# Block 1's left operand from a host-transposed copy of x, and the first keys' transposes three units later

## The chip, the core and the metric

The kernel runs on one core of one Trainium2 chip. The metric is the device time of one execution in microseconds. Engines are named as in the profile: PE (matrix multiply; PEld is its weight load), DVE, ACT, POOL and SP, which here only issues DMAs. "Lnnn" is a line of the kernel before.

## The reference

A decoder block ("block 1": attention of two kinds, then a large mixture of experts) is followed by two more attention layers, on 256 tokens of width 1024. The change touches the start of block 1 alone:

```python
h = rms_norm(x, attn_norm[i])                 # x: 256 x 1024
proj = h @ w_in[i]                            # w_in: 1024 x 3072
mq, mk, mv, dq, dk, dv = jnp.split(proj, split_pts, axis=-1)
mq = apply_rope(rms_norm(mq, q_norm_moba[i]), cos, sin)     # the same for mk, dq, dk
...
x = x + mixed @ w_out[i]                      # mixed: both attentions' outputs
```

## The kernel before

**Units.** Every weight matrix streams through PE in float32 that is split in two parts: `wh` (rounded by ACT, L119) and `wl` (the rest, subtracted by DVE, L129). A unit is 1024 columns of one such pair, and three products (L219 `wh·xh`, L220 `wl·xh`, L221 `wh·xl`) of four 128x512 pieces each, 12 matmuls in all. In block 1, units 0 to 3 make dk (the keys of the second attention), 4 to 7 dq, 8 to 11 mk, 12 to 15 mq, 16 to 19 dv, 20 to 23 mv, and 24 to 31 the output projection. A 1 MB load `raw` holds two units; three `raw` buffers stand, four of `wh` and of `wl`. `Stream.loads` issues the load of chunk c on SP when the parts of chunk c-3 are made. The first chunk comes in four pieces, the second in two, and `after(n)` puts other loads between them.

**The left operand.** x lies with tokens on partitions. `make_xT` transposes it on PE (L270, 16 transposes by the constant `ident`), and ACT (L288) and DVE (L289) make `xh` and `xl` of it with the gain. While these data come, PE runs matmuls on zeros: `busy(15)`, then `busy(36)` behind the first four transposes (`WARM`). The norm of x (`norms`: squares on ACT L247, a chain of 13 small operations on DVE L249, L226 to L233, L465, L466) is only needed after the product, as a scale per token; it ends in `rx` and `rx2`.

**After a product.** `qk` takes a finished dk, dq, mk or mq in two halves of 128 tokens (`part`): ACT squares (L528), DVE multiplies by the rope tables (L532, tiles `mc` and `ms`) and sums the squares (L538), POOL joins the rope (L541, L542). When both halves are there, `norm` runs on POOL: L549, the chain of `rsqrt` (L226 to L236) and, for keys alone, the scaling of `mc` by L557 and L559. Then PE transposes (`tr`, L570, eight 128x128) and ACT copies (L573). `score` (L607) multiplies transposed queries and keys.

**Order.** Each engine runs its own list, in the order in which the program calls. What does not belong to the products is hung on unit numbers, with halves: `self.at(delay, fn)` runs `fn` when the unit counter has moved by `delay`. The table at the head of `block1` holds these numbers: TT the distance from a finished product to its transposes (queries, keys), XS the parts of `xh`, `xl` and the norm, SD the four scores of the second attention, CD the combination of its two maps. With TT = (3, 6), dk, finished when the counter stands at 4, is transposed at 10, and dq, finished at 8, at 11.

Of the kernel before, what the change touches and what calls it, by code (L numbers as in the profile page):

```python
# [18 lines left out]
P = 128  # L19
# [5 lines left out]
REACH = 64  # L25
KA = 16
NCAND = 50
WARM = (15, 36)
CAND = [16 // (a + 1) for a in range(16)]

FIELDS = {}
# [123 lines left out]
class Kernel:  # L155
# [200 lines left out]
    def build(self):  # L356
        tc, nc, A = self.tc, self.nc, self.A
        with (
            tc.tile_pool(name="main", bufs=1) as main,
            tc.tile_pool(name="raw", bufs=3) as raw,  # L360
            tc.tile_pool(name="wgt", bufs=4) as wgt,
            tc.tile_pool(name="ps", bufs=1, space=bass.MemoryType.PSUM) as ps,
            tc.manual_schedule(),
        ):
            self.main = main
            self.pspool = ps

            class _PS:
                @staticmethod
                def tile(shape, dtype, name, tag):  # L370
                    return ps.tile(shape, dtype, name=name, tag=tag, bufs=2 if tag == "s" else 1)

            self.ps = _PS
            x = main.tile([P, 2, 1024], F32, name="x")
            warm = main.tile([P, 1], F32, name="warm")
            nc.vector.memset(warm, 1.0)
            nc.scalar.activation(warm, warm, AF.Copy, scale=warm)

            zero = main.tile([P, 256], F16, name="zero")
            nc.vector.memset(zero, 0.0)  # L380
            idle = self.bank("a0")

            def busy(n):
                for _ in range(n):
                    nc.tensor.matmul(idle[:, 0:256], zero[:, 0:128], zero, start=True, stop=True)

            self.busy = busy
            busy(WARM[0])
            self.consts = [main.tile([P, NFIELD[0]], F32, name="consts0")]
            nc.sync.dma_start(self.consts[0], A["consts0"])  # L390
            xv = A["x"].rearrange("(t p) c -> p t c", p=P)
            nc.sync.dma_start(x[:, :, 0:256], xv[:, :, 0:256])

            srcs = []
            srcs += [A["w_in"][i] for i in range(12)]
            srcs += [A["w_out"][i] for i in range(4)]
            srcs += [A["peer_query"][i] for i in range(8)]
            dn = [A["peer_down"][i] for i in range(64)]
            up = [A["peer_up"][i * 256 : i * 256 + 256, :].rearrange("(j p) d -> p j d", p=P) for i in range(64)]
            srcs += dn[:50] + up[:8] + dn[50:58] + up[8:14] + dn[58:] + up[14:]  # L400
            srcs += [A["a_w_in"][i] for i in range(40)]
            srcs += [A["a_w_out"][i] for i in range(4)]
            srcs += [A["b_w_in"][i] for i in range(16)]
            srcs += [A["b_w_out"][i] for i in range(4)]
            with tc.tile_pool(name="b1c", bufs=1) as pool:
                self.consts.append(pool.tile([P, NFIELD[1]], F32, name="consts1"))

                def after(n):
                    if n == 2:
                        nc.sync.dma_start(self.consts[1], A["consts1"])  # L410
                        return
                    for c in ((1,), (2, 3))[n]:
                        cs = slice(c * 256, c * 256 + 256)
                        nc.sync.dma_start(x[:, :, cs], xv[:, :, cs])

                self.stream = Stream(nc, raw, wgt, srcs, 3, 3, after)
                self.block1(x)
            self.peer(x)
            self.layer_a(x)
            self.layer_b(x)  # L420
# [3 lines left out]
    def block1(self, x):  # L424
        tc, nc, A = self.tc, self.nc, self.A
        ident = self.const("ident")

        TT = (3, 6)
        XS = (1, 1, 1.5, 8)
        SD = (12, 13, 14, 15)  # L430
        CD = (15.5, 15.5, 19.5, 19)
        TD = (18.5, 19, 21, 20.5)
        PD = (20.5, 21, 22, 22)
        FD = (23, 23.5, 24.5, 25.5)
# [10 lines left out]
        with (  # L445
# [3 lines left out]
        ):  # L449
            xh = pl.tile([P, 8, 256], F32R, name="xh1")  # L450
            xl = pl.tile([P, 8, 256], F32R, name="xl1")
            steps = self.make_xT(xh, xl, x, self.small("g_attn"), ahead=0)
            steps[0]()
            self.busy(WARM[1])
            self.stream.prime(1)
# [59 lines left out]
            def qk(key, tabn):  # L515
                n = 64 if "moba" in tabn else 128
                r = 512 // n
                isq = tabn[0] == "q"

                def evac(b0, b1):  # L520
                    ss = pw.tile([P, 2, 8], F32, name=self.nm("ss"), tag="ss")
                    rk = pl.tile([P, 2, 8], F32, name="rk_" + key)
                    tm = pw.tile([P, 2, 8], F32, name=self.nm("tm"), tag="tm")
                    mt = []

                    def part(t, b):
                        sq = pw.tile([P, 512], F32, name=self.nm("sq"), tag="sq")
                        nc.scalar.activation(sq, b, AF.Square)  # L528
                        mc = pw.tile([P, 512], F32, name=self.nm("mc"), tag="mc", bufs=4)
                        ms = pw.tile([P, 512], F32, name=self.nm("ms"), tag="ms")  # L530
                        for dst, kk in ((mc, "c"), (ms, "s")):
                            nc.vector.tensor_tensor(  # L532
                                dst.rearrange("p (r n) -> p r n", n=n),
                                b.rearrange("p (r n) -> p r n", n=n),
                                tabs[tabn, kk][:, t, :].unsqueeze(1).to_broadcast([P, r, n]),
                                op=ALU.mult,
                            )
                        nc.vector.tensor_reduce(ss[:, t, :], sq.rearrange("p (h d) -> p h d", d=64), axis=AX.X, op=ALU.add)  # L538
                        mcv = mc.rearrange("p (h two f) -> p h two f", two=2, f=32)
                        msv = ms.rearrange("p (h two f) -> p h two f", two=2, f=32)  # L540
                        nc.gpsimd.tensor_tensor(mcv[:, :, 0, :], mcv[:, :, 0, :], msv[:, :, 1, :], op=ALU.subtract)  # L541
                        nc.gpsimd.tensor_tensor(mcv[:, :, 1, :], mcv[:, :, 1, :], msv[:, :, 0, :], op=ALU.add)  # L542
                        mt.append(mc)

                    def norm():

                        eng = nc.gpsimd
                        for t in range(2):
                            eng.tensor_scalar(ss[:, t, :], ss[:, t, :], rx2[:, t : t + 1], 0.5 * EPS, op0=ALU.mult, op1=ALU.add)  # L549
                        self.rsqrt(rk, ss, tm, eng)  # L550
                        for t in range(2):
                            if isq:
                                eng.tensor_scalar(
                                    rk[:, t, :], rk[:, t, :], rxs[0][:, t : t + 1], -0.125, op0=ALU.mult, op1=ALU.mult
                                )
                            else:
                                eng.tensor_scalar(rk[:, t, :], rk[:, t, :], rxs[0][:, t : t + 1], None, op0=ALU.mult)  # L557
                                v = mt[t].rearrange("p (h d) -> p h d", d=64)
                                nc.gpsimd.tensor_tensor(  # L559
                                    v, v, rk[:, t, :].unsqueeze(2).to_broadcast([P, 8, 64]), op=ALU.mult  # L560
                                )
                        RW[key] = rk

                    def tr(pp2):
                        def f():
                            pt = self.bank("s")
                            for j in range(2):
                                for t in range(2):
                                    c0 = (2 * pp2 + j) * 128
                                    nc.tensor.transpose(  # L570
                                        pt[:, j * 256 + t * 128 : j * 256 + t * 128 + 128], mt[t][:, c0 : c0 + 128], ident
                                    )
                            nc.scalar.copy(qT[key][:, 2 * pp2 : 2 * pp2 + 2, :].rearrange("p a b -> p (a b)"), pt)  # L573

                        return f

                    part(0, b0)
                    self.at(1, lambda: (part(1, b1), norm()))
                    for p2 in (1, 0):
                        self.at(TT[0] if isq else TT[1], tr(p2), True)  # L580

                return evac

# [1112 lines left out]
def layout(inputs):  # L1696
    i = {k: np.asarray(v) for k, v in inputs.items()}
    a = {}
    a["x"] = np.ascontiguousarray(i["x"][0])
    for n, c in enumerate(_consts(i)):  # L1700
        a[f"consts{n}"] = c
    a["w_in"] = _proj(i["w_in"][0], [4, 3, 1, 0, 5, 2])
# [57 lines left out]
```

## Time and profile before

| | us |
|---|---|
| runs, median of 3 (lowest, highest) | 1468.54 (1466.36, 1471.48) |
| the profiled execution, whole | 1466.31 |
| its span in the profile | 1464.5 |
| PE busy in the span | 1440.2 (98%) |
| PE busy in 10 to 60 us of the span | 43.82 of 50.00 |
| PE busy in 150 us to the end | 1303.98 of 1314.50 |

The profile is one execution. The span's first microseconds are the start of the program; all that the change touches lies in its first 110 us. "Idle before" in square brackets is the time in which an engine had nothing to run, and who released it.

### The profile page before, as it was taken

What the parts mean: (1) busy time and instruction counts of PE and PEld (TensorE: products, weight loads), DVE (VectorE), ACT (ScalarE), POOL (GpSimd) and SP (SyncE); (2) the same over time, 40 slices, a digit from 0 to 9 for tenths busy, and PEclk for the clock granted to TensorE, in tenths of its full rate; (3) what the DMA queues carried; (4) which work ended last, traced back from release to release, by engine and by line L of the source; (5) the groups of instructions that cost most, each with busy time, mean ns of one, the idle gap of its engine ahead of it and who ended that gap; (6) DMA issues with size and microseconds to landing.
All of it is one profiled execution on the core that took longest, in us unless ns stands there. A gap on an engine that the chain in (4) does not pass through costs nothing.

```text
span 1464.5 us, 24829 instructions
## 1 busy us (share of the span) xinstructions
PE 1440.2 (98%) x9375; PEld 1263.0 (86%) x9375; DVE 978.4 (67%) x1985; ACT 888.5 (61%) x1723; POOL 324.5 (22%) x626
## 2 busy tenths in 40 slices
PE   9889999999999999999999999999999999999998
PEld 7677999999999989999878888887888888887887
DVE  6666899996688854456989655556554666666444
ACT  5675554544688854446888544446666666665653
POOL 4760300000133300001333000006333543207300
PEclk9999999999999999999999999999999999999999
DMA  6334445455443355554334555554544454445432
GB/s 251 141 116 150 151 172 194 177 181 190 148 145 124 137 201 182 190 186 163 126 135 143 185 191 200 195 200 179 187 159 166 165 177 168 159 162 181 166 110 86
DMA packets 50935, 243.14 MB, mean 166 GB/s; under 512 B 4224, under 2 KB 11520, under 8 KB 31488
## 3 DMA queue, kind: packets, MB, share of 16 engines
q1 hardware_dynamic: 50528, 241.04, 46.4%
q8 instruction: 73, 1.20, 0.3%
q10 hardware_dynamic: 288, 0.52, 0.1%
q14 instruction: 46, 0.38, 0.1%
HBM read 240.50 MB, written 1.05 MB: 165 GB/s over the span
## 4 chain that ended last, share of the span: by engine, by line
PE 82%; ACT 8%; POOL 4%; DVE 2%; issue 2%; DMA 1%; SPq 0%; ACTq 0%; DVEq 0%; POOLq 0%
PE a L219 14%; PE a L221 14%; PE a L220 14%; PE s L219 10%; PE s L220 9%; PE s L221 9%; ACT o1l L926 4%; ACT wh L119 2%; PE s L1365 2%; PE o L1441 1%; PE o L1449 1%; PE s L1275 1%; DMA raw<-in_w_in_dram 1%; PE t L934 1%; PE o L934 1%
## 5 line engine op out<-in xcount | busy, mean ns | idle before, releaser
L129 DVE TENSOR_TENSOR wl<-raw,wh 128x1024 fp32r<-128x1024 f32 (+1 forms) x435 | 551.5, 1276 | 139.8 <-ACT wh L119 139.7
L119 ACT CAST wh<-raw 128x1024 fp32r<-128x1024 f32 (+1 forms) x435 | 453.0, 1043 | 257.7 <-PE a L221 188.0
L219 PE MATMUL s<-nh,wh 128*128 128x256 f32 x1024 | 292.5, 286 | 0.0
L220 PE MATMUL s<-nl,wh 128*128 128x256 f32 x1024 | 289.6, 283 | 0.0
L221 PE MATMUL s<-nh,wl 128*128 128x256 f32 x1024 | 289.5, 283 | 0.0
L923 POOL TENSOR_TENSOR o1h<-o,ghT 128x256 f16<-128x256 f16 x128 | 85.0, 664 | 561.8 <-DVE o L921 550.8
L219 PE MATMUL a<-wh,gh 128*128 128x512 f32 x512 | 202.4, 395 | 0.0
L221 PE MATMUL a<-wh,gl 128*128 128x512 f32 x512 | 199.4, 390 | 0.0
L220 PE MATMUL a<-wl,gh 128*128 128x512 f32 x512 | 199.3, 389 | 0.0
L219 PEld LDWEIGHTS s<-nh,wh 128*128 128x128 f32 x1024 | 196.9, 192 | 0.1
L220 PEld LDWEIGHTS s<-nl,wh 128*128 128x128 f32 x1024 | 196.4, 192 | 0.1
L221 PEld LDWEIGHTS s<-nh,wl 128*128 128x128 f32 x1024 | 196.2, 192 | 0.0
L926 ACT ACTIVATE o1l<-o,glT 128x64 f16<-128x64 f16 x512 | 146.5, 431 | 29.4 <-DVE o L921 26.4
L219 PE MATMUL a<-wh,xha 128*128 128x512 f32 x320 | 132.4, 414 | 0.5 <-DVE xha L282 0.5
L221 PE MATMUL a<-wh,xla 128*128 128x512 f32 x320 | 125.4, 392 | 0.0
L220 PE MATMUL a<-wl,xha 128*128 128x512 f32 x320 | 125.1, 391 | 0.0
L893 DVE TENSOR_TENSOR gl<-big,gh 128x512 fp32r<-128x512 f32 x64 | 44.3, 693 | 110.4 <-ACT gh L892 110.4
L221 PEld LDWEIGHTS a<-wh,gl 128*128 128x128 f32 x512 | 96.1, 188 | 20.5
L219 PEld LDWEIGHTS a<-wh,gh 128*128 128x128 f32 x512 | 96.6, 189 | 18.6
L220 PEld LDWEIGHTS a<-wl,gh 128*128 128x128 f32 x512 | 96.3, 188 | 18.8
L881 ACT ACTIVATE big<-s 128x512 f32<-128x512 f32 x64 | 38.3, 598 | 98.9 <-PE s L221 98.9
L1370 DVE CUSTOM_DVE_ANT_0 e<-s,bias 128x128 f32<-128x128 f32 (+2 forms) x128 | 34.1, 326 | 70.5 <-PE s L1365 70.5
(409 smaller groups left out, 2588.7 us busy)
## 6 DMA issues: line engine op xcount, KB each, us to landing
raw<-in_peer_down_dram SPq DMA_DIRECT2D x64, 1024.0 KB, 4.8
raw<-in_peer_up_dram SPq DMA_DIRECT2D x64, 1024.0 KB, 4.8
raw<-in_a_w_in_dram SPq DMA_DIRECT2D x40, 1024.0 KB, 4.8
raw<-in_b_w_in_dram SPq DMA_DIRECT2D x16, 1024.0 KB, 4.7
raw<-in_w_in_dram SPq DMA_DIRECT2D x10, 1024.0 KB, 4.9
raw<-in_peer_query_dram SPq DMA_DIRECT2D x8, 1024.0 KB, 4.8
raw<-in_w_out_dram SPq DMA_DIRECT2D x4, 1024.0 KB, 4.8
bias<-in_bias_dram SPq DMA_DIRECT2D x8, 512.0 KB, 5.9
```

The lines of the kernel that those rows point to most:

```text
L119: self.nc.scalar.copy(hi[:, c], self.part(u)[:, c])
L129: eng.tensor_sub(lo[:, c], self.part(u)[:, c], hi[:, c])
L219: nc.tensor.matmul(o, lh, rh, start=start, stop=False)
L220: nc.tensor.matmul(o, lh, rl, start=False, stop=False)
L221: nc.tensor.matmul(o, ll, rh, start=False, stop=stop)
L881: nc.scalar.activation(big[:, sl : sl + 2, :].rearrange("p a b -> p (a b)"), hb, AF.Gelu)
L893: nc.vector.tensor_sub(wl, big[:, sl : sl + 2, :], wh)
L923: nc.gpsimd.tensor_tensor(o1h, o1, b(ghT, H), op=ALU.mult)
L926: nc.scalar.activation(o1l[:, :, i], o1[:, :, i], AF.Copy, scale=glT[:, t : t + 1])
L934: nc.tensor.matmul(o, o2[:, :, i], o1h[:, :, i], start=True, stop=False)
L1365: nc.tensor.matmul(o, l, r, start=start, stop=stop)
L1370: nc.vector.tensor_tensor_reduce(e[:, c], s[:, c], bts[i][:, qt * w : qt * w + w], -1.0, 3.0e38, ALU.add, ALU.min, nmx[g][:, h, qt : qt + 1],)
```

## The change

The host adds an input `xT`, 128 partitions of 8 x 256: x transposed and laid out as `xh` wants it. `make_xT` and its 16 transposes are no longer called in block 1; ACT and DVE read `xT` from its tile in place of PE's banks. `busy(36)` becomes `busy(20)` and stands right behind `busy(15)`. At the head of SP's queue only eight columns of `consts0` stand (the gain); `xT` comes in pieces between the first weights (two, two and four of its eight slices), and x itself and the rest of `consts0` behind the second chunk's pieces and `consts1`. The norm of x moves from 1.5 to 2. dk's transposes move from 6 units after the product to 9; those of mk stay at 6, those of queries at 3. The scores move from (12, 13, 14, 15) to (14, 14.5, 15.5, 16), and `mc` has six buffers in place of four.

```diff
-WARM = (15, 36)
+WARM = (15, 20)
...
-            nc.sync.dma_start(self.consts[0], A["consts0"])
             xv = A["x"].rearrange("(t p) c -> p t c", p=P)
-            nc.sync.dma_start(x[:, :, 0:256], xv[:, :, 0:256])
+            G0, G1 = 128, 136
+            nc.sync.dma_start(self.consts[0][:, G0:G1], A["consts0"][:, G0:G1])
...
+                nc.sync.dma_start(self.xT[:, 0:2, :], xTv[:, 0:2, :])
...
                     if n == 2:
                         nc.sync.dma_start(self.consts[1], A["consts1"])
+                        nc.sync.dma_start(x, xv)
+                        nc.sync.dma_start(self.consts[0][:, 0:G0], A["consts0"][:, 0:G0])
+                        nc.sync.dma_start(self.consts[0][:, G1:], A["consts0"][:, G1:])
                         return
-                    for c in ((1,), (2, 3))[n]:
-                        cs = slice(c * 256, c * 256 + 256)
-                        nc.sync.dma_start(x[:, :, cs], xv[:, :, cs])
+                    ks = (slice(2, 4), slice(4, 8))[n]
+                    nc.sync.dma_start(self.xT[:, ks, :], xTv[:, ks, :])
...
-        TT = (3, 6)
-        XS = (1, 1, 1.5, 8)
-        SD = (12, 13, 14, 15)
-        CD = (15.5, 15.5, 19.5, 19)
+        TT = (3, 9, 6)
+        XS = (1, 1, 2, 8)
+        SD = (14, 14.5, 15.5, 16)
+        CD = (16.5, 17, 19.5, 19)
...
-            steps = self.make_xT(xh, xl, x, self.small("g_attn"), ahead=0)
+            gain = self.small("g_attn")
+
+            def parts(ks):
+                for k in ks:
+                    g = gain[:, k : k + 1]
+                    nc.scalar.activation(xh[:, k, :], self.xT[:, k, :], AF.Copy, scale=g)
+                    nc.vector.scalar_tensor_tensor(xl[:, k, :], self.xT[:, k, :], g, xh[:, k, :], op0=ALU.mult, op1=ALU.subtract)
...
-                        self.at(TT[0] if isq else TT[1], tr(p2), True)
+                        self.at(TT[0] if isq else TT[1] if key == 'dk' else TT[2], tr(p2), True)
```

SP's queue at the program's start, before (`raw_98` is the first chunk of weights, `raw_106` the second, `raw_110` the third; `consts_91` is `consts0`, `consts_97` is `consts1`):

```order
L390 DMA consts_91<-in_consts_dram 128x226
L392 DMA x<-in_x_dram 128x2x256
L96 DMA raw_98<-in_w_in_dram 128x512 x2
...
L414 DMA x<-in_x_dram 128x2x256 x2
L101 DMA raw_106<-in_w_in_dram 128x1024 x2
L410 DMA consts_97<-in_consts_dram 128x1024
L104 DMA raw_110<-in_w_in_dram 128x2048
```

and now (`raw_99`, `raw_106` and `raw_113` are the three chunks, `consts_96` is `consts1`):

```order
L392 DMA consts_91<-in_consts_dram 128x8
L409 DMA xT<-in_xT_dram 128x512
L96 DMA raw_99<-in_w_in_dram 128x512 x2
...
L419 DMA xT<-in_xT_dram 128x1024
L101 DMA raw_106<-in_w_in_dram 128x1024 x2
L413 DMA consts_96<-in_consts_dram 128x1024
L414 DMA x<-in_x_dram 128x2x1024
L415 DMA consts_91<-in_consts_dram 128x128
L416 DMA consts_91<-in_consts_dram 128x90
L104 DMA raw_113<-in_w_in_dram 128x2048
```

Ahead of the third chunk stand now `xT` and x, where x alone stood.

DVE at units 4 and 5, before (`wl_292` is unit 4's, `wl_321` unit 5's, `wl_353` unit 6's; between L249 and L466 lies the norm's chain; `mc_344` is dk's first half):

```order
L129 TENSOR_TENSOR wl_292<-raw_110,wh_272 128x1024
L249 TENSOR_SCALAR ss_280<-ss_280 128x2
...
L466 TENSOR_SCALAR rx_185<-rx_185 128x2
L129 TENSOR_TENSOR wl_321<-raw_110,wh_294 128x1024
L532 TENSOR_TENSOR mc_344<-a_6_218,tab_k_diff_c 128x512
L532 TENSOR_TENSOR ms_345<-a_6_218,tab_k_diff_s 128x512
L538 TENSOR_REDUCE ss_339<-sq_342 128x8
L129 TENSOR_TENSOR wl_353<-raw_226,wh_325 128x1024
```

and now (`wl_255`, `wl_271`, `wl_316` are units 4, 5 and 6):

```order
L129 TENSOR_TENSOR wl_255<-raw_113,wh_235 128x1024
L129 TENSOR_TENSOR wl_271<-raw_113,wh_257 128x1024
L249 TENSOR_SCALAR ss_249<-ss_249 128x2
...
L479 TENSOR_SCALAR rx_160<-rx_160 128x2
L545 TENSOR_TENSOR mc_307<-a_2_193,tab_k_diff_c 128x512
L545 TENSOR_TENSOR ms_308<-a_2_193,tab_k_diff_s 128x512
L551 TENSOR_REDUCE ss_302<-sq_305 128x8
L129 TENSOR_TENSOR wl_316<-raw_201,wh_275 128x1024
```

The norm's chain has changed places with unit 5's `wl`.

PE at unit 10, before (`wh_417` is unit 9, `wh_435` unit 10, `mc_344` and `mc_371` are dk's halves, `mc_454` and `mc_483` dq's):

```order
L221 MATMUL a_32_464<-wh_417,xl_122 128x512
L570 MATMUL s_528<-consts_91,mc_344 128x128
L570 MATMUL s_528<-consts_91,mc_371 128x128
...
L219 MATMUL a_31_463<-wh_435,xh_121 128x512
...
L221 MATMUL a_32_464<-wh_435,xl_122 128x512
L570 MATMUL s_556<-consts_91,mc_454 128x128
L570 MATMUL s_556<-consts_91,mc_483 128x128
```

and now (`wh_398` is unit 10, `wh_430` unit 11, `wh_477` unit 12, `wh_493` unit 13; `mc_417` and `mc_446` are dq's halves, `mc_307` and `mc_334` dk's):

```order
L221 MATMUL a_24_427<-wh_398,xl_125 128x512
L583 MATMUL s_507<-consts_91,mc_417 128x128
L583 MATMUL s_507<-consts_91,mc_446 128x128
...
L219 MATMUL a_23_426<-wh_430,xh_124 128x512
...
L221 MATMUL a_36_550<-wh_477,xl_125 128x512
L583 MATMUL s_567<-consts_91,mc_307 128x128
L583 MATMUL s_567<-consts_91,mc_334 128x128
...
L219 MATMUL a_35_549<-wh_493,xh_124 128x512
```

dk's transposes have moved behind unit 12; dq's stand where they stood, behind unit 10. POOL's list holds the same operations in the same order as before.

## Rows read from the trace of the kernel before

**Rows 1.** Chain of waits, first 60 us: start us, us, what.

```profile
8.47 9.99 DMA raw<-in_w_in_dram
...
30.18 0.74 POOL mc L541
...
45.04 1.43 PE s L570 x7
```

**Rows 2.** Timeline of PE: start us, us, operation, [idle before and its releaser].

```profile
25.86 0.50 PE L220 MATMUL a<-wl,xh 128*128 128x512 f32 x1 [1.62 <-DVE wl L129]
...
32.05 0.50 PE L220 MATMUL a<-wl,xh 128*128 128x512 f32 x1
...
39.89 0.39 PE L221 MATMUL a<-wh,xl 128*128 128x512 f32 x1
43.62 0.33 PE L570 MATMUL s<-consts,mc 128*128 128x128 f32 x1 [3.34 <-POOL mc L559]
45.04 1.43 PE L570 MATMUL s<-consts,mc 128*128 128x128 f32 x7 [1.08 <-POOL mc L559]
46.12 0.78 PE L219 MATMUL a<-wh,xh 128*128 128x512 f32 x1
...
50.23 1.03 PE L570 MATMUL s<-consts,mc 128*128 128x128 f32 x8
51.02 0.47 PE L219 MATMUL a<-wh,xh 128*128 128x512 f32 x1
...
75.57 0.98 PE L570 MATMUL s<-consts,mc 128*128 128x128 f32 x7 [0.77 <-POOL mc L559]
...
80.30 0.98 PE L570 MATMUL s<-consts,mc 128*128 128x128 f32 x7 [0.54 <-POOL mc L542]
```

**Rows 3.** Stretches: us, busy (instructions) of PE, PEld, DVE, ACT, POOL; PEclk, DMA share, GB/s.

```profile
0.00:1.50 1.50, 0.43 (x3) 0.31 (x4) 0.22 (x2) 0.78 (x1) 0.19 (x4) 1.00 0.00 0
...
0.00:8.80 8.80, 7.73 (x56) 6.46 (x57) 2.14 (x6) 3.54 (x6) 0.19 (x4) 1.00 0.62 193
8.80:16.40 7.60, 7.60 (x41) 6.46 (x40) 5.88 (x12) 5.47 (x11) 0.60 (x1) 1.00 1.04 414
...
40.00:46.00 6.00, 1.58 (x9) 1.11 (x8) 2.27 (x2) 0.35 (x1) 5.73 (x7) 0.95 0.48 175
46.00:49.00 3.00, 3.00 (x10) 2.43 (x9) 0.94 (x1) 1.76 (x3) 2.82 (x5) 0.53 0.02 5
```

**Rows 4.** DMAs issued between 8 and 9 us: size, us to landing.

```profile
raw<-in_w_in_dram SPq DMA_DIRECT2D x1, 1024.0 KB, 10.0
```

**Rows 5.** Timeline of ACT at the third chunk.

```profile
19.50 1.06 ACT L247 ACTIVATE sq<-x 128x1024 f32<-128x1024 f32 x1
...
21.73 1.03 ACT L119 CAST wh<-raw 128x1024 fp32r<-128x1024 f32 x1
```

**Rows 6.** Timeline of DVE at units 4 to 6.

```profile
21.86 0.45 DVE L249 TENSOR_SCALAR ss<-ss 128x2 f32<-128x2 f32 x1 [0.73 <-ACT sq L247]
...
24.59 1.22 DVE L129 TENSOR_TENSOR wl<-raw,wh 128x1024 fp32r<-128x1024 f32 x1
25.72 0.68 DVE L532 TENSOR_TENSOR mc<-a,tab_k_diff_c 128x512 f32<-128x512 f32 x1
```

**Rows 7.** Timeline of POOL, from dk's second half to the end of dq's rope.

```profile
30.18 0.74 POOL L541 TENSOR_TENSOR mc<-mc,ms 128x256 f32<-128x256 f32 x1 [0.68 <-DVE ms L532]
...
36.89 0.22 POOL L230 TENSOR_TENSOR tm<-rk_dk 128x16 f32<-128x16 f32 x1
37.19 1.08 POOL L231 TENSOR_TENSOR tm<-tm,ss 128x16 f32<-128x16 f32 x1
...
47.00 0.74 POOL L542 TENSOR_TENSOR mc<-mc,ms 128x256 f32<-128x256 f32 x1
```

**Rows 8.** Timeline of DVE, the split parts of units 11 and 12.

```profile
39.90 2.37 DVE L129 TENSOR_TENSOR wl<-raw,wh 128x1024 fp32r<-128x1024 f32 x2
```

More of the change, by code (lines that the diff above doesn't have):

```diff
@@ L406, in build @@
                 self.consts.append(pool.tile([P, NFIELD[1]], F32, name="consts1"))
+                self.xT = pool.tile([P, 8, 256], F32, name="xT")
+                xTv = A["xT"].rearrange("p (k t) -> p k t", k=8)
+                nc.sync.dma_start(self.xT[:, 0:2, :], xTv[:, 0:2, :])
                 def after(n):
@@ L451, in block1 @@
             xl = pl.tile([P, 8, 256], F32R, name="xl1")
-            steps = self.make_xT(xh, xl, x, self.small("g_attn"), ahead=0)
+            gain = self.small("g_attn")
[4 more added lines that the diff above has]
+                    nc.vector.scalar_tensor_tensor(xl[:, k, :], self.xT[:, k, :], g, xh[:, k, :], op0=ALU.mult, op1=ALU.subtract)
+            steps = [lambda kk=kk: parts((2 * kk, 2 * kk + 1)) for kk in range(4)]
             steps[0]()
@@ L528, in part @@
                         nc.scalar.activation(sq, b, AF.Square)
-                        mc = pw.tile([P, 512], F32, name=self.nm("mc"), tag="mc", bufs=4)
+                        mc = pw.tile([P, 512], F32, name=self.nm("mc"), tag="mc", bufs=6)
                         ms = pw.tile([P, 512], F32, name=self.nm("ms"), tag="ms")
@@ L1699, in layout @@
     a["x"] = np.ascontiguousarray(i["x"][0])
+    a["xT"] = np.ascontiguousarray(i["x"][0].T.reshape(8, P, 256).transpose(1, 0, 2)).reshape(P, 2048)
     for n, c in enumerate(_consts(i)):
```

## Prediction, made before the changed kernel was run

> **What bounds the kernel now.** I read the page first: PE is busy for 1440.2 of 1464.5 us, and from 150 us on for 1303.98 of 1314.50. Where PE has no holes, a shift made earlier is carried to the end unchanged, so only the first 110 us matter. There I followed the chain of waits [rows 1]. It does not run through PE. It runs from the load of the third weight chunk (issued at 8.47, landed at 18.47 [rows 4]) over ACT's `wh` and DVE's `wl` of unit 4, DVE's norm and dk's two halves, to POOL at 30.18; from there POOL alone holds it until 45.04, when dk's scaled keys are ready and PE can transpose them. PE's timeline shows what that costs [rows 2]: after 40.28 (39.89 + 0.39) PE waits 3.34 us, does one transpose, waits 1.08 us more. Then the table of stretches shows a second price [rows 3]: PE, busy 1.58 of 6.00 us from 40 to 46, has a granted clock of 0.53 from 46 to 49, close to the lower of its two levels (1.2 of 2.4 GHz). Unit 10 therefore takes from 46.12 to 50.23, 4.11 us, where 34 matmuls from 32.05 to 39.89 took 0.23 us each, 2.77 a unit: 1.34 us lost.
>
> So the question is not when PE starts, but when POOL is through with what PE's next transposes need.
>
> **The start.** Removed are 16 transposes and 16 matmuls on zeros, and ACT and DVE no longer wait for PE's banks. PE could then end units 0 to 3 some microseconds earlier. None of this reaches the end, because unit 4 needs the third chunk. What counts is when that lands. Before, 0.12 MB of constants, 1.05 of x, two chunks of 1.05, 0.52 of `consts1` and the chunk itself, 4.84 MB, had to pass; the stretches give 193 GB/s x 8.80 us + 414 GB/s x 7.60 us = 4.85 MB by 16.40 [rows 3], and landing followed 2.1 us behind. Now x comes twice, as `xT` ahead of the weights and as x ahead of the third chunk: 5.89 MB. The extra megabyte at 414 GB/s is 2.5 us. Against it stands the slow first stretch, 193 GB/s: there x came in rows of 1 KB and the constants in rows of 904 bytes, and these are now rows of 2 and 4 KB, besides the gain's short ones. No row shows this mix at the start, so I bound it. If the rate by bytes stays, the first 1.58 MB (gain, half of `xT`, first chunk) end at 8.4 instead of 8.8 for 1.69 MB, 4.2 MB at 414 GB/s take 10.1 us, the short rest of `consts0` perhaps 0.5: 19.0 instead of 16.4, that is +2.6. If the first pieces run at 414 GB/s from 1.5 us on (before that nothing moved [rows 3]), they end at 5.3 and the chunk at 16.0: -0.4. If the start is limited by the number of rows, 896 in place of 1152 over 7.3 us, they end at 7.2 and the chunk at 17.9: +1.5. I take +1.6 us for this delay, called d, because the low rate and the short rows stand together and end together in the trace, and keep -0.4 to +2.6. What hides the earlier start is thus this very load; were it to land as early as the lower end, d would only vanish, not turn into a gain.
>
> The Trainium skill, page "DMA: Bandwidth & Descriptors", section "Specifications", holds that transfers of 512 bytes and more already run at line rate. By that rule 1 KB rows were not what made the first stretch slow, the low rate would belong to the start itself, d would be +2.6, and the sum below +3.0 instead of +2.0 us; the rows show that the rate was low as long as the short rows were in the queue, but not which of the two made it so.
>
> **The norm on DVE.** Before, DVE began the norm's chain at 21.86, when ACT's squares of x were done, and unit 5's `wl` came behind it at 24.59; dk's first half began at 25.72 [rows 6]. Now `wl` of unit 5 comes first. It needs ACT's `wh`, which comes behind the squares, at 21.73 to 22.76 [rows 5]. So DVE starts it at 22.78, is through at 23.91 (1.13, from 24.59 to 25.72), runs the chain (24.59 - 21.86 = 2.73) to 26.64, and starts dk's first half there instead of at 25.72: 0.92 us later, whatever the load does. Behind it the order of DVE is that of before. POOL's second half of dk thus starts at 30.18 + 0.92 + d = 32.7. The wait of 1.62 us for unit 5's `wl` [rows 2] gets shorter by this, but PE then waits for unit 6's, and unit 7 resumes 0.92 + d later than at 32.05, so nothing of it is kept.
>
> **dk's and dq's transposes.** dk's no longer stop PE at unit 10, and here the wait of 4.42 us and its clock go. But what is late next is dq: its transposes stay behind unit 10, and POOL reaches dq's rope only when dk's norm and scaling are done. In the trace POOL works without a hole from 30.18 to 47.74 (47.00 + 0.74), the end of dq's rope, 17.56 us [rows 7], and its list is unchanged. I add c for one more collision: POOL's L231 took 1.08 instead of about 0.22 us where DVE split a chunk [rows 7], and the two splits of 39.90 to 42.27 [rows 8] are now followed by a third, unit 13's, since PE no longer stands at unit 9 and ACT goes on. That is 0.86 us; I take 0.9, bounds 0 and 1.0. So dq's rope ends at 30.18 + 0.92 + 1.6 + 17.56 + 0.9 = 51.2. PE is there at 43.0 + 0.92 + 1.6 = 45.6 (40.28 and one unit more, plus the shift) and waits some 5 us, at dq instead of dk. After that seven transposes and the start of unit 11 take 1.08 us as before (45.04 to 46.12): unit 11 starts at 52.2, before at 51.02, **+1.2**. The clock's 1.34 us, paid before in unit 10, is then paid in unit 11: **+1.3** (bounds 0, if PE keeps its clock, and 1.3; I take the row, since the idle time is no shorter).
>
> **Behind it.** dk's eight transposes now come after unit 12 and cost what dq's did, 50.23 to 51.02: **+0.8**. The scores keep their number and length; they are only later, while dq's norm is done earlier than they need it. mk's second half no longer queues on DVE behind a score, and PE comes to mk's transposes two scores later, so the waits of 0.77 and 0.54 us at 75.57 and 80.30 [rows 2] should go: **-1.3**. Six buffers of `mc` cost nothing: with four, mk would have waited for dk's transposes. What lies beyond is hung on PE's units and shifts with it.
>
> **Sum.** +1.2 + 1.3 + 0.8 - 1.3 = +2.0 us; as a formula d + c + clock - 1.8. With all lower ends it is -2.2, with all upper ends +3.1. The profiled execution took 1466.31 us, which gives 1468.3; the runs' median is 2.2 above it, so the forecast for a median is 1468.54 + 2.0 = 1470.5 us, 1466.3 to 1471.7 by the terms alone.
>
> **Rivals.** First, **PE is freed at unit 10 and stays free**. This is what it would be if POOL had dq's rope ready when PE arrives at 45.6: unit 11 starts at 46.4, 4.6 us earlier than before, less 0.8 for dk's transposes, plus 1.3 behind: 5.1 us, 1463.4. For it speaks that dk's and dq's joined wait is 4.42 us now and that about a third of POOL's 17.56 us looks like collisions, operations of 1 us among like ones of 0.2. Against it: POOL would have to be 5.6 us faster on an unchanged list, with DVE splitting no less. It decides from 2.4 us less on POOL for a gain over 0.3%. I give it 8%.
>
> Second, **the third chunk lands much later**: every microsecond of its landing goes through ACT, DVE and POOL to PE's end one for one, with no slack on the way. The queue now holds x and two loads of short rows ahead of it, and it has shown a lag of 2.1 us between last byte by the rates and landing; should the short rows and the following chunk, which is in the queue at the same time, cost 3 us more than I took, d is 4.6 and the time 1473.5. It is slower by over 0.3% from d = 4.0 on, a landing at 22.5 instead of 18.5. Against it: 414 GB/s in the busy stretch, and only 256 short rows. I give it 15%.
>
> Third, inside the forecast, PE keeps its clock and the load is not late: 1466.3 to 1468, no change either.
>
> **How the numbers follow.** 0.3% is 4.4 us, about what a measurement of this kernel can tell from no change. Forecast 77% (within 0.3%), first rival 8% (faster), second 15% (slower). The range reaches over the terms' ends and by about 2 us further on both sides, for the spread of the runs (1466.36 to 1471.48) and the near parts of the rivals: 1465.0 to 1474.0.
>
> **What would show it.** Right: PE starts unit 0 earlier but waits 3 us or more ahead of unit 4; the third chunk lands at about 20; DVE runs unit 5's `wl` ahead of the norm; the wait at unit 10 is at dq's transposes, released by POOL's rope, 4 to 6 us; the clock is low behind it; no wait at mk's and mq's. Wrong: no wait over 2 us at dq's transposes (first rival), or a landing behind 22 (second).

## The result, and the profile after

The changed kernel took 1474.69 us in the median of 7 runs (1473.35 to 1479.93); the kernel before, run on the same chip, 1467.80 (7 runs). The ratio is 1.0052, 95% interval 1.0034 to 1.0070: about 7.6 us slower, where the prediction said 1470.5 and a range up to 1474.0. The profiled execution has a span of 1472.9 us (before 1464.5), and all of the difference is there by the first transposes of the next block (L270): they stand at 140.88 before and at 149.01 after, 8.13 us later. From there on the two traces take 1323.6 and 1323.9 us. That position is used below as a second measure, since it leaves out what happens behind the change. Ahead of it lie some 35 us whose work no kernel here alters, and in which the granted clock fell in some traces and not in others (see the last section). So the table further down also gives the point where that stretch begins: the end of a wait of 2.0 us at the transposes of a combination (L654), which every trace has in the same length. It ends at 105.39 before and at 113.52 after, again 8.13 us later.

The loads of the third chunk, from the trace after (size, us to landing; it was issued at 9.32), and the unit's first cast on ACT (start us, us, operation, [idle before and releaser]); they answer to [rows 4, 5]:

```profile
raw<-in_w_in_dram SPq DMA_DIRECT2D x1, 1024.0 KB, 12.2
```

```profile
21.58 1.05 ACT L119 CAST wh<-raw 128x1024 fp32r<-128x1024 f32 x1 [5.80 <-DMA raw<-in_w_in_dram]
```

The chunk landed at 21.5 instead of 18.5. Stretches of the trace after (us, busy of PE, PEld, DVE, ACT, POOL, PEclk, DMA share, GB/s), to be held against [rows 3]:

```profile
0.00:8.80 8.80, 7.73 (x42) 5.83 (x43) 3.25 (x8) 5.01 (x9) 0.19 (x4) 1.00 0.70 216
8.80:16.40 7.60, 6.04 (x26) 4.37 (x25) 4.98 (x10) 4.42 (x9) 0.34 (x1) 0.98 1.01 382
16.40:19.00 2.60, 2.60 (x8) 2.04 (x7) 0.64 (x1) 0.00 (x0) 2.60 (x4) 0.50 1.03 414
52.00:58.00 6.00, 5.35 (x18) 4.57 (x19) 0.31 (x1) 2.72 (x4) 4.63 (x19) 0.57 0.13 53
87.00:93.00 6.00, 6.00 (x25) 4.99 (x25) 5.24 (x11) 3.57 (x6) 5.16 (x11) 0.72 0.76 270
```

216 x 8.8 + 382 x 7.6 + 414 x 2.6 give 5.88 MB by 19.0 us, about the 5.89 that had to pass, so by these rates the chunk's last byte passed there; landing followed 2.5 us behind. The last two rows show the granted clock well below full speed twice, behind two waits of PE. DVE, the norm and dk's first half, answering to [rows 6]:

```profile
25.83 1.23 DVE L129 TENSOR_TENSOR wl<-raw,wh 128x1024 fp32r<-128x1024 f32 x1 [1.95 <-ACT wh L119]
26.97 0.16 DVE L249 TENSOR_SCALAR ss<-ss 128x2 f32<-128x2 f32 x1
...
29.41 0.69 DVE L545 TENSOR_TENSOR mc<-a,tab_k_diff_c 128x512 f32<-128x512 f32 x1
```

The norm's chain now stands behind unit 5's `wl`, and dk's first half starts 3.69 us later than in [rows 6]. POOL, from dk's second half to the end of dq's rope, answering to [rows 7]:

```profile
33.86 0.73 POOL L554 TENSOR_TENSOR mc<-mc,ms 128x256 f32<-128x256 f32 x1 [0.68 <-DVE ms L545]
...
44.44 2.00 POOL L572 TENSOR_TENSOR mc<-mc,rk_dk 128x512 f32<-128x512 f32 x1
46.43 2.32 POOL L570 TENSOR_SCALAR rk_dk<-rk_dk,rx 128x8 f32<-128x8 f32 x1
...
51.87 0.72 POOL L555 TENSOR_TENSOR mc<-mc,ms 128x256 f32<-128x256 f32 x1
```

That is 18.73 us, where 17.56 were before; two operations of about 1.0 and 0.3 us took 2.00 and 2.32 while DVE split three chunks. PE, answering to [rows 2]:

```profile
51.29 0.47 PE L583 MATMUL s<-consts,mc 128*128 128x128 f32 x1 [3.37 <-POOL mc L555]
52.65 1.75 PE L583 MATMUL s<-consts,mc 128*128 128x128 f32 x7 [0.89 <-POOL mc L555]
54.05 0.77 PE L219 MATMUL a<-wh,xh 128*128 128x512 f32 x1
...
61.04 1.03 PE L583 MATMUL s<-consts,mc 128*128 128x128 f32 x8
...
80.38 1.04 PE L583 MATMUL s<-consts,mc 128*128 128x128 f32 x8
...
84.34 0.27 PE L583 MATMUL s<-consts,mc 128*128 128x128 f32 x1
86.82 0.98 PE L583 MATMUL s<-consts,mc 128*128 128x128 f32 x7 [2.21 <-POOL mc L555]
```

At 51.29 is the predicted wait for dq, at 61.04 dk's transposes without a wait, at 80.38 mk's without a wait. At 86.82 is what the prediction did not have: the wait at mq's transposes has not gone from 0.54 us, it has become 2.21. ACT and DVE ahead of it:

```profile
79.59 0.49 ACT L641 ACTIVATE e<-e,bq,rk_dq 128x128 f32<-128x128 f32 x1 [2.20 <-DVE bq L633]
...
81.74 0.58 ACT L541 ACTIVATE sq<-a 128x512 f32<-128x512 f32 x1
```

```profile
79.60 1.22 DVE L129 TENSOR_TENSOR wl<-raw,wh 128x1024 fp32r<-128x1024 f32 x1
80.73 0.16 DVE L656 RECIPROCAL rden<-den 128x2 f32<-128x2 f32 x1
...
82.96 0.69 DVE L545 TENSOR_TENSOR mc<-a,tab_q_moba_c 128x512 f32<-128x512 f32 x1
```

On ACT the four exponentials of the fourth score (79.59 to 81.74) stand ahead of the square of mq's second half; on DVE the first two combinations (80.73 to 82.96) stand ahead of its products. Both were moved there by the change (SD from 15 to 16, CD from 15.5 to 16.5 and 17).

The shift of 8.13 us is thus: unit 11 starts 3.03 later (51.02, now 54.05); up to mk's transposes 2.82 are added (units 11 and 12 at the low clock, 6.99 us instead of 5.54; dk's transposes 0.8; the second score, half a unit behind the first, 0.4; 0.2 of small change); mk's wait gives 1.0 back; mq's costs 1.68; and the stretch behind it, 4.45 us before, takes 6.05 at a clock of 0.72: 1.60.

### The profile page after: what moved, and what is told of

Read it like the earlier page. It is cut to its first block, busy times and chain, and to the rows that moved or that the text cites. A ratio compares the mean times of both kernels' runs of the same rounds, so it can differ in the third digit from the quotient of the medians.

```text
span 1472.9 us, 24770 instructions
## 1 busy us (share of the span) xinstructions
PE 1443.7 (98%) x9343; PEld 1264.0 (86%) x9343; DVE 977.9 (66%) x1985; ACT 889.0 (60%) x1723; POOL 323.1 (22%) x626
## 4 chain that ended last, share of the span: by engine, by line
PE 83%; ACT 8%; POOL 3%; DVE 2%; issue 2%; DMA 1%; SPq 0%; ACTq 0%; DVEq 0%; POOLq 0%
PE a L219 15%; PE a L221 14%; PE a L220 14%; PE s L219 9%; PE s L220 9%; PE s L221 9%; ACT o1l L939 4%; ACT wh L119 2%; PE s L1378 2%; PE o L1454 1%; PE o L1462 1%; DMA raw<-in_w_in_dram 1%; PE s L1288 1%; PE o L947 1%; PE t L947 1%
```

## The experiments

Twelve kernels were run, on three chips; the ratio is to the kernel before on the same chip, so kernels of different chips are better compared by it than by their medians. "Waits" are PE's idle times at the transposes ahead of unit 11 or 12 and at mq's second half. The waits and the last two columns come from one traced execution each; the last two are the end of the 2.0 us wait and the start of the next block's first transposes.

| kernel | median us | ratio (95%) | wait, dk or dq | wait, mq | 2.0 us wait ends at | next block at |
|---|---|---|---|---|---|---|
| before | 1466.6 to 1467.8 | 1 | 3.34 + 1.08 | 0.54 | 105.39 | 140.88 |
| changed | 1474.69 | 1.0052 (1.0034, 1.0070) | 3.37 + 0.89 | 2.21 | 113.52 | 149.01 |
| start_only | 1472.01 | 1.0024 (1.0011, 1.0037) | 3.35 + 1.09 | 0.51 | 108.30 | 143.77 |
| sched_only | 1472.26 | 1.0028 (1.0015, 1.0040) | 4.45 + 1.03 | 2.18 | 108.11 | 145.14 |
| cd_late | 1478.73 | 1.0067 (1.0051, 1.0083) | 3.37 + 0.88 | 3.87 (combination) | 115.00 | 152.05 |
| cd_old | 1477.12 | 1.0067 (1.0047, 1.0087) | 3.41 + 1.03 | 2.04 | 112.67 | 148.15 |
| sd_early | 1477.40 | 1.0072 (1.0057, 1.0087) | 4.40 + 1.03 | 2.89 | 114.12 | 149.60 |
| sd_cd | 1474.60 | 1.0047 (1.0030, 1.0063) | 4.43 + 0.88 | 0.47 | 110.77 | 146.24 |
| x_late | 1473.24 | 1.0040 (1.0026, 1.0054) | 4.45 + 0.88 | 2.18 | 109.34 | 146.37 |
| tt_late | 1469.19 | 1.0024 (1.0013, 1.0035) | 0 | 2.89 | 107.90 | 143.38 |
| fill_waits | 1471.68 | 1.0034 (1.0022, 1.0046) | 1.17 + 1.03, filled | 0.26, filled | 110.42 | 147.49 |
| all_three | 1467.67 | 1.0005 (0.9993, 1.0017) | 0.25 | 2.89 | 101.65 | 138.69 |
| all_four | 1462.20 | 0.9959 (0.9945, 0.9974) | 0.26 | 0.47 | 99.21 | 136.27 |
| tables_only | 1462.66 | 0.9965 (0.9951, 0.9979) | 0.26 | 0.47 | 98.83 | 137.43 |

**The two parts alone: start_only and sched_only.** The first has `xT`, the loads, WARM and XS as changed, and of the tables the old ones; the second the reverse:

```diff
 # start_only, against the changed kernel
-        TT = (3, 9, 6)
-        SD = (14, 14.5, 15.5, 16)
-        CD = (16.5, 17, 19.5, 19)
+        TT = (3, 6, 6)
+        SD = (12, 13, 14, 15)
+        CD = (15.5, 15.5, 19.5, 19)
 # and mc with four buffers
```

> The start part alone: xT, the order of the loads, WARM and XS as changed; TT, SD, CD and the buffers of mc as before. Theory (the shift of dk's first half on DVE, 3.69 us in the changed kernel's trace, goes through POOL to PE one for one, nothing else changes behind it): dk's transposes and unit 11 come 3.7 us later than before, and the time is 3.5 to 4.2 us above before, about 1472. Rival 1 (the start is all): 6.5 to 7 us above before. Rival 3 (the start's earlier units are worth something): below before.

> The schedule part alone: TT, SD, CD and the buffers of mc as changed; the start as before. Theory: unit 11 starts 0.3 to 0.7 us earlier than before (POOL starts dk's second half at 30.2 as before and needs 17.6 to 18.7 us; PE waits some 5 us at dq's transposes), then come the clock 1.3, dk's transposes 0.8, the scores 0.4, mk -1.0, mq +1.7, the clock behind it +1.6: 4 to 5 us above before, about 1472.5. Rival 1 (the start is all): within 1 us of before.

0.24% and 0.28%, 3.5 and 4.1 us; together 7.6, as much as both at once within the intervals. So the rival that the start is all falls. By the end of the 2.0 us wait the two parts are 2.91 and 2.72 us later than before, together 5.6 of the 8.13; of the rest, 1.60 is the low clock behind mq's wait, which the changed kernel's trace has and the traces of the parts do not: in sched_only's the clock stayed at 1.00 behind mq's wait (84 to 90 us) and fell behind the 2.0 us wait instead. In start_only the third chunk's first cast is at 21.25, so that it landed some 2.7 us later than before, and unit 10 starts at 49.80 instead of 46.12, 3.7 later, as expected; 0.8 of it comes back by the end of the 2.0 us wait, since unit 10 takes 3.74 us here instead of 4.11 and mk's wait is 0.39 instead of 0.77:

```profile
48.39 1.76 PE L583 MATMUL s<-consts,mc 128*128 128x128 f32 x7 [1.09 <-POOL mc L572]
49.80 0.78 PE L219 MATMUL a<-wh,xh 128*128 128x512 f32 x1
```

In sched_only unit 11 starts at 49.57, 1.45 us earlier than before (0.3 to 0.7 had been expected), and the wait at mq is there with the old start too:

```profile
48.17 1.75 PE L570 MATMUL s<-consts,mc 128*128 128x128 f32 x7 [1.03 <-POOL mc L542]
49.57 0.78 PE L219 MATMUL a<-wh,xh 128*128 128x512 f32 x1
...
83.03 0.98 PE L570 MATMUL s<-consts,mc 128*128 128x128 f32 x7 [2.18 <-POOL mc L542]
```

**What holds mq: cd_late, cd_old, sd_early, sd_cd.** The first theory took DVE's combinations for the cause and moved them alone, behind mq's second half or back to their old place:

```diff
-        CD = (16.5, 17, 19.5, 19)
+        CD = (17.5, 17.5, 19.5, 19)      # cd_late
+        CD = (15.5, 15.5, 19.5, 19)      # cd_old
```

> The changed kernel, its first two combinations (CD) moved from 16.5 and 17 to 17.5, so that on DVE they stand behind mq's second half instead of ahead of it. Theory (the queue on DVE made mq's transposes late, and the idle PE then lost its clock): the wait of 2.21 us at mq's transposes goes, the units behind it run at full clock, and the time falls by 3 to 4 us against the changed kernel, to about 1471. Rival 1 (all of the loss is the start: the late third chunk): the time stays at that of the changed kernel, within 1 us. Rival 2 (POOL itself is late, whatever DVE does): the wait stays over 1 us.

> The changed kernel, CD put back to the old 15.5 and 15.5. DVE is idle for 2.69 us there in the changed kernel's trace (73.81 to 76.50), and the combinations take 2.2. Theory: as with the later place, the wait at mq's transposes goes and 3 to 4 us come back, to about 1471; if the combinations in that hole push mq's first half, up to 0.5 us less. Rival 1 (start alone): no change.

Both expectations failed: by the ratios neither kernel became faster than the changed one, and by the end of the 2.0 us wait cd_late is 1.5 us behind it. In cd_old the wait is 2.04 us. DVE in cd_old shows why:

```profile
83.71 0.69 DVE L545 TENSOR_TENSOR mc<-a,tab_q_moba_c 128x512 f32<-128x512 f32 x1 [1.53 <-ACT sq L541]
```

DVE has nothing left to do for 1.53 us, and still the product waits, for ACT's square of the same half (83.10 to 83.68), which comes behind the exponentials of the fourth score. In cd_late PE's new wait stands at the transposes of the combination, which now came late itself:

```profile
86.17 0.83 PE L667 MATMUL t<-consts,e 128*128 128x128 f32 x3 [3.87 <-DVE e L659]
```

That the product waits for a square that it does not read agrees with the Trainium skill, page "PSUM — Partial Sum Buffer", section "PSUM bank collisions raise a hardware error": two engines may not read one bank at the same time, and the compiler orders them. That the order was made here for this reason, no run shows. So the scores were moved instead:

```diff
-        SD = (14, 14.5, 15.5, 16)
+        SD = (14, 14.5, 15, 15.5)        # sd_early
```

> The changed kernel, its last two scores moved from 15.5 and 16 to 15 and 15.5; the combinations stay at 16.5 and 17. Moving the combinations alone did not take away the wait at mq's transposes: in those traces DVE's products of mq wait for ACT's square of the same half, and that square stands behind the four exponentials of the fourth score, at 16.5. New theory (ACT's exponentials of the fourth score, not DVE's combinations, hold mq's second half): with that score half a unit earlier mq's square is done before PE needs it, the wait of 2.21 us at mq's transposes goes or falls under 0.6, the clock stays up behind it, and the time falls by 3 to 4 us against the changed kernel, to about 1471. Rival (DVE as a whole is the limit there, or POOL): the wait stays over 1.5 us.

This failed too: 2.89 us at mq. ACT's square is now done early (78.72 to 79.3), but DVE has the combinations ahead of the product, as in the first theory:

```profile
82.94 0.75 DVE L659 SCALAR_TENSOR_TENSOR e<-e,rden,e 128x128 f32<-128x128 f32 x2
83.60 0.68 DVE L545 TENSOR_TENSOR mc<-a,tab_q_moba_c 128x512 f32<-128x512 f32 x1
```

So there were two queues, each of them enough. sd_cd takes both away:

```diff
-        SD = (14, 14.5, 15.5, 16)
-        CD = (16.5, 17, 19.5, 19)
+        SD = (14, 14.5, 15, 15.5)
+        CD = (15.5, 15.5, 19.5, 19)      # called behind the scores of the same half unit
```

> The changed kernel with both edits of the earlier runs at once: scores 3 and 4 at 15 and 15.5, and the first two combinations at 15.5 right behind the fourth score. Theory (two queues hold mq's second half, ACT's exponentials and DVE's combinations, and each alone suffices, so that taking away one showed nothing): the wait at mq's transposes, 2.2 us in the changed kernel and 2.0 to 2.9 in the runs with one edit, goes, and the time falls by 3 to 4 us against the changed kernel, to about 1471. Rival (POOL or PE itself sets it): the wait stays over 1.5 us.

```profile
84.93 0.27 PE L583 MATMUL s<-consts,mc 128*128 128x128 f32 x1
85.67 0.98 PE L583 MATMUL s<-consts,mc 128*128 128x128 f32 x7 [0.47 <-POOL mc L555]
```

The wait falls to 0.47, the clock behind it stays at 1.00 (85 to 91 us), and the next block comes 2.77 us earlier than in the changed kernel. By the runs alone the gain, expected at 3 to 4 us, is not shown: 1.0047 against 1.0052, with intervals that overlap almost wholly. The clearer pair for the same edit is all_three and all_four, below.

**The load: x_late.** x and the rest of the first constants are issued behind the third chunk, the squares of x half a unit later:

```diff
+                if c == 2:
+                    self.after(3)        # x and the rest of consts0, no longer in after(2)
...
-        XS = (1, 1, 2, 8)
+        XS = (1, 1, 2.5, 8)
```

> The changed kernel, x and the rest of the first constants loaded behind the third weight chunk instead of ahead of it, and the norm's squares half a unit later, behind unit 5's cast. Theory (the megabyte ahead of the third chunk is what makes it land 3.0 us later, and every microsecond of that goes through DVE and POOL to PE): the third chunk lands at 18.3 to 19, dk's first half starts 2.5 to 3 us earlier, dq's rope ends as much earlier, and the time falls by 2.5 to 3.5 us against the changed kernel. Rival (the landing is set by the low rate of the first 8 us and the number of transfers, not by the bytes ahead): it lands behind 20.5 and the time falls by less than 1 us.

ACT and POOL in x_late:

```profile
18.35 2.00 ACT L121 CAST wh<-raw 128x1024 fp32r<-128x1024 f32 x2 [2.79 <-DMA raw<-in_w_in_dram]
```

```profile
30.18 0.74 POOL L558 TENSOR_TENSOR mc<-mc,ms 128x256 f32<-128x256 f32 x1 [0.69 <-DVE ms L549]
```

The chunk lands at 18.2, 3.2 us earlier, POOL starts dk's second half at 30.18 to the hundredth where it started before [rows 7], and dq's transposes follow 3.8 us earlier (48.81). Of this 3.2 us are the load's; the rest goes with the norm's squares, whose place moved in the same run. mq's wait (2.18) and the clock behind it (0.72) are as in the changed kernel, and the 2.0 us wait ends 4.2 us earlier. The next block comes only 2.64 us earlier, because behind that wait the clock was 0.72 here and 1.00 in the changed kernel. The ratios differ by 1.8 us, less than expected, and their intervals overlap: the trace shows the gain, the times do not.

**POOL's chain: tt_late.** dk's transposes at counter 12, dq's at 13:

```diff
-        TT = (3, 9, 6)
+        TT = (3, 8, 6, 5)                # the fourth for dq
...
```

> The changed kernel, dk's transposes one unit earlier (8 units after the product, counter 12) and dq's two units later (5, counter 13). Theory (POOL's chain, which ends dq's rope at 52.6 us, costs PE 4.3 us of waits at unit 11 and 1.3 us of clock behind it, and units 11 and 12 could run in that time): both waits go and the time falls by 4 to 5.5 us against the changed kernel, to about 1470. Rival (the gain is eaten by the next wait: mk's or mq's norm on POOL, which is not earlier): PE arrives earlier at mq's transposes and waits there so much longer; the time falls by less than 2 us.

Both waits are gone, units 11 and 12 run at full clock in the time (PEclk 1.00 from 46 to 52), and the next block comes 5.63 us earlier; the median falls by 5.5, by the ratios 4.1, both in the expected range. POOL's chain is no shorter here (dq's rope ends at 51.9); PE only has other work.

**The clock: fill_waits.** Matmuls on zeros, 30 ahead of dq's transposes and 18 ahead of mq's, into a free bank:

```diff
+                    if isq:
+                        self.at(TT[0], lambda: self.fill(30 if key == 'dq' else 18), True)
...
```

> The changed kernel with matmuls on zeros put on PE ahead of dq's transposes (30) and ahead of mq's (18), in the time in which PE waits there; nothing waits for them, and they end before the awaited data is there. Theory (the units behind the two waits are slow because PE's clock fell while it stood): units 11 and 19 run at full clock, 1.3 and 1.6 us come back, and the time falls by 2 to 3 us against the changed kernel, the waits themselves staying. Rival (the slow units have another cause, late weights or contention): the time stays the same, and the units keep 4.1 us and more.

PE in fill_waits:

```profile
45.66 3.45 PE L392 MATMUL o<-zero 128*128 128x256 f16 x30
50.28 0.33 PE L590 MATMUL s<-consts,mc 128*128 128x128 f32 x1 [1.17 <-POOL mc L562]
...
82.81 2.14 PE L392 MATMUL o<-zero 128*128 128x256 f16 x18
84.79 0.27 PE L590 MATMUL s<-consts,mc 128*128 128x128 f32 x1
85.32 0.98 PE L590 MATMUL s<-consts,mc 128*128 128x128 f32 x7 [0.26 <-POOL mc L562]
```

The 2.0 us wait ends 3.1 us earlier than in the changed kernel, and the time falls by 3.0 us in the medians, 2.6 by the ratios, in the expected range, though the intervals of the ratios overlap. In this trace the filling kept the clock behind mq (1.00 from 85 to 91), but not behind dq, where 1.17 and 1.03 us of waiting were left over: unit 11 is slow there (0.60 from 53 to 57). Over the whole execution the mean granted clock was 0.997 in 7 of 12 executions; in none of the 7 of the changed kernel was it above 0.995. This speaks for the theory; the trace shows it for one of the two places, and the times alone do not decide it.

**Together: all_three, all_four, tables_only.** all_three is tt_late, x_late and sd_early at once; all_four adds the combinations' place of sd_cd.

> The three edits together on the changed kernel. If each is its own stretch of the path and nothing new comes up behind: about 10 us below the changed kernel, some 1465, a little below before. If the waits follow on one another (POOL's chains of mk and mq are as long as dk's and dq's and have no slack left): 4 to 6 us below the changed kernel, not below before.

> The kernel with three edits (dk's transposes at 12 and dq's at 13, x behind the third chunk, scores 3 and 4 half a unit earlier), and the first two combinations behind the fourth score at 15.5 as well. In the trace with three edits one wait of 2.89 us was left, at mq's transposes, and DVE's combinations stood ahead of mq's second half there. Theory: it goes, 2.5 to 4 us, to 1463 to 1465, below before. Rival (the next wait comes up in its place): within 1 us of the kernel with three edits.

all_three gives back the loss, 7.0 us in the medians and 6.9 by the ratios, which lies between its two expectations, but is not told apart from before; its one large wait is mq's 2.89. all_four takes that away, PE's two places are

```profile
46.28 0.98 PE L587 MATMUL s<-consts,mc 128*128 128x128 f32 x7 [0.26 <-POOL mc L576]
...
74.14 0.98 PE L587 MATMUL s<-consts,mc 128*128 128x128 f32 x7 [0.47 <-POOL mc L559]
```

and the kernel is 0.41% faster than before (0.26 to 0.55), 6.0 us by the ratio and 4.4 in the medians. The next block comes 2.42 us earlier than in all_three, as much as mq's wait fell; the median falls by 5.5. The clock is a candidate for the rest, which no run isolates: the mean granted clock was 0.997 or above in 3 of 12 executions of all_three and 0.998 in 5 of 7 of all_four. tables_only then keeps the old start, x transposed on PE, and has all_four's tables:

> The kernel before with its old start (x transposed on PE, no xT), and the schedule alone as in the kernel with four edits: dk's transposes at 12, dq's at 13, scores at 14, 14.5, 15, 15.5, the combinations behind the fourth. POOL began dk's second half at 30.18 us before and also in the run with x behind the third chunk. Theory (the start sets POOL's beginning and nothing else; the transposed copy is worth nothing as long as the third chunk lands no earlier): the time is that of the kernel with four edits, within 1 us. Rival (the earlier first units are worth something once PE no longer waits for POOL): over 1.5 us above it.

0.9965 against 0.9959: the same within the intervals. In the traces the 2.0 us wait ends at 98.83 here and at 99.21 in all_four; that the next block comes 1.16 us later is a clock that fell once more, behind a wait of 1.85 us at 127.02 (0.72 in the 6 us from there). With x late enough not to delay the third chunk, the transposed copy costs nothing and, in these runs, brings nothing.

## Why the prediction was wrong

**What held.** PE was not freed at unit 10; the wait moved to dq's transposes and was 3.37 + 0.89 us there, released by POOL's rope (predicted some 5). The clock behind it fell, and units 11 and 12 lost 1.45 us (predicted 1.3). dk's transposes cost 0.79 (0.8). mk's wait went (1.0 with its small change). The first units started earlier, unit 0 by 1.91 us (7.17 instead of 9.08), and it was worth nothing. The norm's new place cost DVE 0.66 us beside the load (0.92). One sign failed without a price: PE waited only 0.54 us ahead of unit 4, not 3 or more, as it had already waited 1.33 us ahead of 14.26 and run at a granted clock of 0.50 from 16.4 to 19.0 us.

**"The start".** The size of d was wrong: taken at 1.6 us with an upper end of 2.6, it was 3.0. By 8.8 us 1.90 MB had passed (216 GB/s); the other 3.99 of the 5.89 MB would have ended at 18.4 at 414 GB/s, 2.0 us later than before. The second stretch ran at 382 instead of 414 GB/s, 0.6 more, and landing took 2.5 us behind the last byte instead of 2.1, 0.4 more. That the upper end named 19.0 for the last byte was met by its sum and not by its terms. The mistake was the choice inside the bounds: the low rate of the first stretch was put down to its short rows. (Added up again, the bound by rows is 17.8 and +1.4, not 17.9 and +1.5.) Two slices of it, before and then after (columns as in [rows 3]), show what longer rows changed:

```profile
1.50:3.50 2.00, 2.00 (x11) 1.44 (x10) 0.00 (x0) 0.80 (x2) 0.00 (x0) 1.00 0.81 238
3.50:8.80 5.30, 5.30 (x46) 4.71 (x45) 1.92 (x4) 1.97 (x4) 0.00 (x0) 1.00 0.72 230
...
1.50:3.50 2.00, 2.00 (x11) 1.44 (x10) 0.00 (x0) 0.80 (x2) 0.00 (x0) 1.00 0.54 114
3.50:8.80 5.30, 5.30 (x32) 4.08 (x31) 3.03 (x6) 3.43 (x7) 0.00 (x0) 1.00 0.96 317
```

From 3.5 to 8.8 us the rate rose from 230 to 317 GB/s, but the DMA engines were busy for 0.72 of that time before and for 0.96 now: per busy time they moved 319 and 330 GB/s. While they worked, then, the stretch with rows of 1 KB in it was hardly slower than the one with rows of 2 and 4 KB. That agrees with the Trainium skill, page "DMA: Bandwidth & Descriptors", section "Specifications", as the prediction quoted it. Why the engines stood still for part of the time before, no run shows. From 1.5 to 3.5 us, where the gain's rows of 32 bytes now stand first, 114 GB/s passed instead of 238: a loss that the prediction named no price for, and whose cause no run isolates. Together with c (1.17 instead of 0.9) and seven transposes at the lower clock (1.40 instead of 1.08 us), less 0.26 for the norm, unit 11 came 3.03 us later instead of 1.2: 1.8 us of the miss. x_late gives the early landing back by moving x and the rest of the first constants behind the third chunk; whether by their bytes (1.16 MB, 2.8 us at 414 GB/s) or also by their short rows, it does not separate.

**"Behind it".** Here is the larger part. The step said that mk's and mq's waits "should go", for 1.3 us, and checked only PE's order and mk's place on DVE. For mq the change itself had put the fourth score (SD 16) and two combinations (CD 16.5 and 17) between mq's halves, on ACT and on DVE, and neither list was read there. Instead of -1.3 us this stretch gave -1.0 + 1.68 + 1.60 = +2.3: 3.6 us of the miss. The 1.60 is the low clock of the traced execution, and it is the part that changes from one execution to the next (see the last section). sched_only shows the wait without the start's delay, sd_cd and all_four show that it goes when both queues are cleared. The second score, half a unit behind the first, cost 0.4 us that the step had at nothing ("keep their number and length").

1.8 + 3.6 + 0.4 and 0.3 of small change are the 6.1 us between +2.0 and the trace's +8.1; over all runs the kernel was about 7.6 us slower.

**The rivals.** The second, the load much later, was priced alone: its point of decision, d = 4.0, was never reached. The time came out in its region because a smaller d met a new wait. No rival had a new wait behind dq; that was the gap in the list.

## What to carry to other kernels

When a table of due times is moved, read each engine's own list between the two halves of every later step that something waits for, not only the list of the engine that was meant to gain. A wait can stand behind two queues at once; then taking away either shows nothing, and only both together do. And a load that holds up the start should not stand behind data that is needed later than it, whatever form these data come in.

## What was not expected of the hardware

Waits of the same length cost PE its clock in one execution and not in another. After 2.0 to 2.9 us of waiting at mq's transposes the granted clock of the next 6 us was 0.72 in the changed kernel, in sd_early and in x_late, and 0.50, the lower of its two levels (1.2 of 2.4 GHz) throughout, in tt_late, but 1.00 in cd_old, sched_only and all_three. The clearest case is the wait that no kernel alters, here in the trace before and in x_late:

```profile
105.39 0.55 PE L654 MATMUL t<-consts,e 128*128 128x128 f32 x3 [2.01 <-ACT pT L656]
...
109.34 0.55 PE L671 MATMUL t<-consts,e 128*128 128x128 f32 x3 [2.00 <-ACT pT L673]
```

In the 6 us from there the clock was 1.00 in eight of the fourteen traces and 0.72 in six (sched_only, x_late, fill_waits, all_three, all_four, tables_only). To the next block it takes 35.5 us in the traces before, changed, start_only, cd_old, sd_early, sd_cd and tt_late, and 37.0 to 37.1 in the others, of which cd_late lost its 1.6 us only behind a later wait of 1.8 us; tables_only lost it behind both and takes 38.6. So one such wait can move a trace of this kernel by 1.5 us that have nothing to do with what was changed.

The executions of one kernel lie accordingly: start_only's at 1469.2 to 1469.7 us with a mean granted clock of 0.997, at 1471.6 to 1473.2 with 0.993 or 0.994, at 1474.6 to 1475.6 with 0.991 or 0.992. What decides it in an execution, no run here shows.
